# State matmuls of the SSD branch from split operands, with the operands made ahead and some work of TensorE placed elsewhere

## The chip, the cores and the metric

The kernel runs on one core of a Trainium2 chip. The metric is the device time of one execution in microseconds, as the median of several runs. One further execution is profiled; its trace has every instruction of every engine with its start and its length, and every statement on where time goes refers to that execution.

## The reference

Two layers of a hybrid encoder on 512 tokens of width 1024, all in float32. Each layer projects the residual stream x once and feeds three branches (a bidirectional Mamba-2 scan, differential attention, cross-attention into 256 memory tokens); each branch is projected back, weighted by a gate computed from x, and summed. The change touches only the first branch, and of it only the states between chunks and the order of work:

```python
# one direction; chunks of Q = 128 tokens, 32 heads in 4 groups, state width N = 128
decay_states = jnp.exp(a_cum[..., -1:] - a_cum)
states = jnp.einsum('bcqgn,bgrcq,bcqgrp->bcgrpn', bm, decay_states, xs)
chunk_decay = jnp.moveaxis(jnp.exp(a_cum[..., -1]), -1, 0)
def step(h, inp):
    s_c, d_c = inp
    return h * d_c[..., None, None] + s_c, h
_, prev = lax.scan(step, h0, (jnp.moveaxis(states, 1, 0), chunk_decay))
y_off = jnp.einsum('bcqgn,bcgrpn,bgrcq->bcqgrp', cm, prev, jnp.exp(a_cum))
```

Here `xs` is the convolved x times the step `dt`, `bm` and `cm` are the convolved B and C, and `prev` is the state in front of each chunk. It is computed forward and backward.

## The kernel before, in words

**Split operands.** Most products are made of float32 values split in two: a rounded high part h (the type `F32R`, which TensorE takes in a single pass) and the rest l. `split` makes them: ScalarE copies x to h, VectorE subtracts h from x. `mm3` then runs three matmuls, l by h, h by l and h by h, into one PSUM bank. A plain `mm` of float32 operands is one instruction in the program and two in the trace.

**Units.** The layer's weights come in units of 128 x 1024, one DMA each on the SP queue. A unit is loaded, split (`wh` on ScalarE, `wl` on VectorE) two units ahead, and used by 24 matmuls of 128 x 512 into one PSUM bank of the pool `pj`, or two banks of 12 for the branch output. `U(unit, ...)` puts a unit into TensorE's order and, in the middle of it, small pieces of other work; `J(...)` puts such a piece between units. TensorE's order is the written one; the order on the other engines is set by a scheduler that goes by priorities and its own estimates, and `late(-n)` raises the priority of what stands within.

**One group of the scan** (8 heads; g = 0 to 3) consists of:

- `bu`, `cu`, `xu(g, 0..3)`: projections of B, C and four slices of x, each convolved over five taps: one operation on ScalarE and four on VectorE (`acc`), then a SiLU on ScalarE (`bC`, `cC`, `xsC`).
- `bturn`, `xturn(g, b)`: four transposes on TensorE into the one bank of the pool `pt`, copied out by ScalarE to `bT` and `xsT`.
- `states(g, part)`, part 0 to 2: the forward state of chunk `part` and the backward one of chunk 3 - `part`. VectorE multiplies `xsT` by the weights `wst` (`xw`), TensorE multiplies that by `bT`, and the running state `prev` takes it up (ScalarE for part 0, two VectorE operations later).
- `expos(g, b)`: for two heads, tables of decays are loaded into one of two buffers (`ab`), masked on VectorE, put through eight exponentials on ScalarE, summed and multiplied by the products of B and C to give `m`; the decays `eb` are loaded as well.
- `block(g, b)`: matmuls of `prev` with `cC` and of `xsT` with `m`, then some VectorE work to the gated, split output `yh`, `yl`.
- `wu(g, 0..3)`: the branch's output projection, summed into `mrg`.
- `zu` are the units of the SiLU gate z. `gu` are early units of the branch gates: a tanh into `tg`, which is stored to DRAM for later.

While group g is projected, the blocks of the group before run in between. In what follows, the "first group" of the loop is g = 1, beside which the blocks of group 0 run.

Of the kernel before, what the change touches and what calls it, by code (L numbers as in the profile page):

```python
# [12 lines left out]
F32R = mybir.dt.float32r  # L13
# [7 lines left out]
P = 128  # L21
S = 512
# [29 lines left out]
class Net:  # L52
# [391 lines left out]
    def ssd(self, l):  # L444
# [22 lines left out]
        def bturn(g):  # L467
            pt = self.bank(self.pt, "pt")
            for c in range(4):
                self.tr(pt[:, c * P:(c + 1) * P], G["bC", g][:, c * P:(c + 1) * P])  # L470
            G["bT", g] = self.t(self.sp, [P, S], "bT")
            self.act(G["bT", g], pt)

        def cpart(g, ps=None):
            def f(wh, wl):
# [30 lines left out]
        def xturn(g, b):  # L506
# [2 lines left out]
                self.tr(pt[:, c * P:(c + 1) * P], xc[:, c * P:(c + 1) * P])  # L509
            self.act(G["xsT", g][:, :, b * P:(b + 1) * P], pt.rearrange("p (c e) -> p c e", c=4))  # L510

        def states(g, part):

            sp = self.sp
            for d, c in ((0, part), (1, 3 - part)):
                hs = slice(d * 32 + g * 8, d * 32 + g * 8 + 8)
                old = G.get(("prev", g, d, c))
                xw = self.t(sp, [P, 8, 64], "xw", bufs=2)
                self.tt(xw, G["xsT", g][:, c, :].rearrange("p (h e) -> p h e", h=8),
                        bc(self.wst[:, c, hs, None], [P, 8, 64]), ALU.mult)  # L520
                ps = self.bank(self.pm, "pm")
                self.mm(ps, G["bT", g][:, c * P:(c + 1) * P], xw)
                pv = self.t(sp, [P, 8, 64], f"prev{d}{c}")
                psv = ps.rearrange("p (h e) -> p h e", h=8)
                if old is None:
                    self.act(pv, psv)
                else:
                    self.tt(pv, old.rearrange("p (h e) -> p h e", h=8),
                            bc(self.dtot[:, c, hs, None], [P, 8, 64]), ALU.mult)
                    self.tt(pv, pv, psv, ALU.add)  # L530
                G["prev", g, d, c + 1 if d == 0 else c - 1] = pv.rearrange("p h e -> p (h e)")

        def zpart(g, b):
            def f(wh, wl):
# [104 lines left out]
        def gate(i, j, t=None):  # L639
            def f(wh, wl):  # L640
                ps = yield from self.proj2(wh, wl)
                o = self.t(self.sp, [P, S], "tg", bufs=2) if t is None else t()
                self.act(o, ps, AF.Tanh, scale=0.5, bias=self.hgb[:, 8 * i + j:8 * i + j + 1])
                if t is None:
                    d = self.dgt[i, j] = self.t(self.dp, [P, S], f"dgt{i}{j}")
# [96 lines left out]
        U(gu())  # L742
        J(xturn, 0, 3)
        J(expos, 0, 0)
        U(gu())
        J(states, 0, 0)
        U(zu(0, 0), (states, 0, 1))
        for g in range(1, 4):
            p = g - 1
            U(bu(g))  # L750
            if g == 1:
                J(states, 0, 2)
                U(zu(p, 1), (block, p, 0))
            else:
                J(block, p, 0)
                U(zu(p, 1))
            J(expos, p, 1)
            U(cu(g))
            U(gu())
            J(block, p, 1)  # L760
            U(xu(g, 0), (bturn, g))
            J(expos, p, 2)
            U(zu(p, 2), (within, g))
            U(xu(g, 1))
            J(block, p, 2)
            J(xturn, g, 0)
            U(zu(p, 3))
            J(expos, p, 3)
            U(xu(g, 2))
            J(xturn, g, 1)  # L770
            J(block, p, 3)
            U(xu(g, 3))
            U(gu(), (xturn, g, 2))
            U(wu(p, 0))
            J(xturn, g, 3)
            U(wu(p, 1))
            U(wu(p, 2), (states, g, 0))
            J(states, g, 1)
            U(wu(p, 3))
            J(states, g, 2)  # L780
            J(expos, g, 0)
            U(zu(g, 0))

        for b in range(4):
            U(gate(0, 4 + b, place(4 + b)))
# [645 lines left out]
```

## Time and profile before

| | |
|---|---|
| median of 3 runs | 2189.69 us |
| lowest and highest | 2188.62 and 2190.12 us |
| the profiled execution | 2190.09 us |
| its span, first to last instruction | 2188.3 us |
| busy, share of the span | TensorE 98%, VectorE 71%, ScalarE 53%, GpSimd 3% |
| granted TensorE clock, mean | 0.997 |
| HBM read and written | 126 GB/s |

A row of the timeline gives start and length in microseconds, engine, source line, operation, out<-in with partitions and elements, how many instructions are merged, and in brackets the idle time before it and what ended that. L99 is the line of `mm`, L77 of `tt`, L80 of `stt`, L87 of `act` and L107 of `tr`, all helpers, so the names of the tiles tell which step it is. Matmuls overlap: the length of one is longer than the step from its start to the next one's start. In a row of groups the columns are count, busy time, mean length in nanoseconds, and idle time before.

### The profile page before, as it was taken

The numbers are of one execution on the slowest core, as the hardware profiler recorded it, in microseconds if no ns is written. First come the engines' busy times: TensorE is split into PE (matmuls) and PEld (weight loads), VectorE is DVE, ScalarE is ACT, GpSimd is POOL, SyncE is SP. The second block draws the span as 40 slices with busy tenths as digits, with TensorE's granted clock in tenths as the row PEclk, the third lists the DMA queues.
The fourth block names the chain that finished last, engine by engine and source line by source line (L and its number), as shares of the span: only waits on it lengthen the run. The fifth ranks groups of instructions, "written<-read, shape, count | busy, mean of one in ns | idle before, by whom it ended". The sixth has DMA issues, their size and how long they took to land.

```text
span 2188.3 us, 29240 instructions
## 1 busy us (share of the span) xinstructions
PE 2148.1 (98%) x11122; PEld 1787.3 (82%) x11122; DVE 1546.6 (71%) x2404; ACT 1152.1 (53%) x2035; POOL 61.3 (3%) x38
## 2 busy tenths in 40 slices
PE   8999999999999999999999999999999999999998
PEld 6787878788888888887888777878788888888876
DVE  5677777869554788766566677878675547888667
ACT  5676757554432455543345676858533325555430
POOL 0010101010000000000000000101000000000000
PEclk9999999999999999999999999999999999999999
DMA  4654545454554433324564654545444334333253
GB/s 162 159 148 136 163 122 169 121 144 149 173 168 123 137 113 107 112 83 153 153 208 128 164 148 135 165 134 160 127 135 135 106 113 130 112 111 107 91 160 111
DMA packets 111984, 299.46 MB, mean 137 GB/s; under 512 B 12716, under 2 KB 13284, under 8 KB 111588
## 3 DMA queue, kind: packets, MB, share of 16 engines
q1 hardware_dynamic: 111844, 297.60, 46.0%
q8 instruction: 87, 1.43, 0.3%
q14 instruction: 53, 0.43, 0.1%
HBM read 257.16 MB, written 19.43 MB: 126 GB/s over the span
## 4 chain that ended last, share of the span: by engine, by line
PE 78%; DVE 9%; DMA 7%; ACT 2%; issue 2%; SPq 0%; DVEq 0%; ACTq 0%
PE pj L99 61%; PE pm L99 14%; DMA ab<-dab 4%; PE pt L107 2%; DVE acc L80 2%; DVE wl L77 2%; DMA wr<-wu 2%; DVE y L77 1%; DMA fth<-rd 1%; DVE eb L77 1%; ACT wh L87 1%; DVE ab L77 1%; ACT L87 1%; DVE y L80 1%; DMA mkv<-dkv 0%
## 5 line engine op out<-in xcount | busy, mean ns | idle before, releaser
L99 PE MATMUL pj<-xh,wl 128*128 128x512 f32 x1664 | 668.3, 402 | 0.2 <-DVE wl L77 0.2
L99 PE MATMUL pj<-xh,wh 128*128 128x512 f32 x1664 | 652.5, 393 | 8.1 <-ACT xh L87 6.0
L99 PE MATMUL pj<-xl,wh 128*128 128x512 f32 x1664 | 652.0, 392 | 0.0
L77 DVE TENSOR_TENSOR wl<-wr,wh 128x1024 fp32r<-128x1024 f32 x330 | 403.6, 1224 | 154.8 <-ACT wh L87 154.2
L87 ACT ACTIVATE wh<-wr 128x1024 fp32r<-128x1024 f32 x330 | 347.5, 1054 | 248.4 <-PE pj L99 169.5
L99 PEld LDWEIGHTS pj<-xh,wh 128*128 128x128 f32 x1664 | 314.0, 189 | 76.1 <-ACT xh L87 6.0
L99 PEld LDWEIGHTS pj<-xh,wl 128*128 128x128 f32 x1664 | 314.0, 189 | 70.8 <-issue 6.7
L99 PEld LDWEIGHTS pj<-xl,wh 128*128 128x128 f32 x1664 | 314.5, 189 | 65.0 <-issue 2.9
L87 ACT ACT_TABLE_LOAD x107 | 137.3, 1283 | 93.4 <-DVE ab L77 31.7
L87 ACT ACTIVATE ab<-ab,bias 128x128 f32<-128x128 f32 x512 | 161.3, 390 | 14.6 <-DVE ab L77 13.8
L80 DVE SCALAR_TENSOR_TENSOR acc<-pj,pr,acc 128x510 f32<-128x510 f32 (+1 forms) x192 | 142.2, 744 | 32.6 <-ACT acc L87 31.7
L77 DVE TENSOR_TENSOR ab<-ab,cst 128x1024 f32<-128x1024 f32 x64 | 78.2, 1223 | 72.9 <-DMA ab<-dab 72.8
L1059 DVE TENSOR_REDUCE fmx<-pm 128x1 f32<-128x512 f32 x128 | 85.0, 685 | 46.8 <-PE pm L99 46.8
L99 PE MATMUL pj<-yh,wl 128*128 128x512 f32 x256 | 106.1, 415 | 0.5 <-DVE mrg L77 0.5
L87 ACT ACTIVATE fpp<-pm,fmx 128x512 f32<-128x512 f32 x128 | 87.1, 685 | 33.8 <-DVE fmx L1059 33.8
L99 PE MATMUL pj<-dy,wh 128*128 128x512 f32 (+1 forms) x384 | 102.6, 356 | 0.9 <-DVE dy L77 0.9
L99 PE MATMUL pj<-yl,wh 128*128 128x512 f32 x256 | 100.2, 391 | 0.1
L99 PE MATMUL pj<-yh,wh 128*128 128x512 f32 x256 | 99.8, 390 | 0.0
L77 POOL TENSOR_TENSOR sqa<-sqa,sz 128x512 f32<-128x512 f32 x32 | 60.1, 1878 | 887.6 <-ACT sz L87 887.6
L99 PE MATMUL pj<-cy,wh 128*128 128x512 f32 x256 | 78.8, 389 | 0.0
L99 PEld LDWEIGHTS pj<-dy,wh 128*128 128x128 f32 x384 | 67.5, 188 | 13.2 <-DVE dy L77 2.1
L99 PE MATMUL pj<-wh,xl 128*128 128x256 f32 x256 | 73.3, 286 | 0.0
(274 smaller groups left out, 3309.2 us busy)
## 6 DMA issues: line engine op xcount, KB each, us to landing
wr<-wu SPq DMA_DIRECT2D x336, 512.0 KB, 3.7
ab<-dab SPq DMA_DIRECT2D x64, 512.0 KB, 5.6
eb<-deb SPq DMA_DIRECT2D x64, 256.0 KB, 5.9
mkv<-dkv SPq DMA_DIRECT2D x16, 512.0 KB, 4.1
rsw<-rx SPq DMA_DIRECT2D x64, 128.0 KB, 2.3
dy<-dy SPq DMA_DIRECT2D x32, 256.0 KB, 2.3
dgt<-tg SPq DMA_DIRECT2D x24, 256.0 KB, 3.9
dkv<-mo SPq DMA_DIRECT2D x16, 256.0 KB, 4.4
```

Source lines behind the costliest of these rows:

```text
L77: (eng or self.nc.vector).tensor_tensor(out=out, in0=a, in1=b, op=op)
L80: self.nc.vector.scalar_tensor_tensor(out=out, in0=a, scalar=s, in1=b, op0=op0, op1=op1)
L87: self.nc.scalar.activation(out=out, in_=a, func=f, **kw)
L99: self.nc.tensor.matmul(out=out, lhsT=a, rhs=b, start=first, stop=last)
L107: self.nc.tensor.transpose(out=out, in_=x, identity=self.ident)
L1059: nc.vector.tensor_reduce(out=mx[:, c:c + 1], in_=ps, axis=AX.X, op=ALU.min)
```

## The change

The states are no longer multiplied as plain float32. `bturn` splits the transposed B into `bTh` and `bTl`, out of the PSUM bank. A new function `weighted` makes the weighted x of both directions (in a tile of the tag `y`, which `block` uses too) and splits it into `xwh` and `xwl`, two buffers each; it stands ahead of `states` with raised priority, for part 0 behind the last transposes of the group's x, for parts 1 and 2 at the end of the part before. `states` then runs `mm3`, three single passes for each direction.

The pieces also stand elsewhere in the units. Each part of the states is now in the middle of a unit of its own, where two of three had shared a place or stood between units. The transposes of x stand later: those of slice 0 behind the z unit, of slice 1 in the middle of the last x projection, of slice 2 behind the gate unit. One early gate has gone from the last group's (g = 3) place behind `cu` to the start, ahead of the states of group 0; there are as many units as before. `tg` has one buffer instead of two.

```diff
@@ bturn
-            G["bT", g] = self.t(self.sp, [P, S], "bT")
-            self.act(G["bT", g], pt)
+            G["bT", g] = [self.t(self.sp, [P, S], n, F32R) for n in ("bTh", "bTl")]
+            self.split(*G["bT", g], pt)
@@
+        def ends(part):
+            return (0, part), (1, 3 - part)
+
+        def weighted(g, part):
+
+            with self.late(-LN):
+                for d, c in ends(part):
+                    hs = slice(d * 32 + g * 8, d * 32 + g * 8 + 8)
+                    xh, xl = G["xw", g, d] = [self.t(self.sp, [P, S], n, F32R, bufs=2) for n in ("xwh", "xwl")]
+                    xw = self.t(self.sp, [P, S], "y", bufs=2)
+                    self.tt(xw.rearrange("p (h e) -> p h e", h=8),
+                            G["xsT", g][:, c, :].rearrange("p (h e) -> p h e", h=8),
+                            bc(self.wst[:, c, hs, None], [P, 8, 64]), ALU.mult)
+                    self.split(xh, xl, xw)
+
         def states(g, part):
...
-            for d, c in ((0, part), (1, 3 - part)):
+            for d, c in ends(part):
...
-                xw = self.t(sp, [P, 8, 64], "xw", bufs=2)
-                self.tt(xw, G["xsT", g][:, c, :].rearrange("p (h e) -> p h e", h=8),
-                        bc(self.wst[:, c, hs, None], [P, 8, 64]), ALU.mult)
                 ps = self.bank(self.pm, "pm")
-                self.mm(ps, G["bT", g][:, c * P:(c + 1) * P], xw)
+                self.mm3(ps, *(t[:, c * P:(c + 1) * P] for t in G["bT", g]), *G.pop(("xw", g, d)), True, True)
...
+            if part < 2:
+                weighted(g, part + 1)
@@ gate
-                o = self.t(self.sp, [P, S], "tg", bufs=2) if t is None else t()
+                o = self.t(self.sp, [P, S], "tg") if t is None else t()
@@ the order
         J(expos, 0, 0)
+        J(weighted, 0, 0)
         U(gu())
-        J(states, 0, 0)
+        U(gu(), (states, 0, 0))
         U(zu(0, 0), (states, 0, 1))
         for g in range(1, 4):
             p = g - 1
-            U(bu(g))
+            U(bu(g), *(((states, 0, 2),) if g == 1 else ()))
             if g == 1:
-                J(states, 0, 2)
                 U(zu(p, 1), (block, p, 0))
             else:
                 J(block, p, 0)
                 U(zu(p, 1))
             J(expos, p, 1)
             U(cu(g))
-            U(gu())
-            J(block, p, 1)
-            U(xu(g, 0), (bturn, g))
+            if g < 3:
+                U(gu())
+                J(block, p, 1)
+            U(xu(g, 0), *(((block, p, 1),) if g == 3 else ()), (bturn, g))
             J(expos, p, 2)
             U(zu(p, 2), (within, g))
             U(xu(g, 1))
             J(block, p, 2)
+            U(zu(p, 3))
             J(xturn, g, 0)
-            U(zu(p, 3))
             J(expos, p, 3)
             U(xu(g, 2))
-            J(xturn, g, 1)
             J(block, p, 3)
-            U(xu(g, 3))
-            U(gu(), (xturn, g, 2))
+            U(xu(g, 3), (xturn, g, 1))
+            U(gu())
+            J(xturn, g, 2)
             U(wu(p, 0))
             J(xturn, g, 3)
+            J(weighted, g, 0)
             U(wu(p, 1))
             U(wu(p, 2), (states, g, 0))
-            J(states, g, 1)
-            U(wu(p, 3))
-            J(states, g, 2)
+            U(wu(p, 3), (states, g, 1))
             J(expos, g, 0)
-            U(zu(g, 0))
+            U(zu(g, 0), (states, g, 2))
```

The states on TensorE, part 0 of g = 1 in layer 0, in the middle of the third output unit. Before:

```order
L99 MATMUL pj_1540<-yh_875,wh_1462 128x512
L99 MATMUL pj_1540<-yl_876,wh_1462 128x512
L99 MATMUL pm_1557<-xw_1555,bT_1077 128x512
L99 MATMUL pm_1563<-xw_1561,bT_1077 128x512
L99 MATMUL pj_1541<-yh_875,wl_1463 128x512
L99 MATMUL pj_1541<-yh_875,wh_1462 128x512
```

and now:

```order
L99 MATMUL pj_1627<-yl_949,wh_1537 128x512
L99 MATMUL pm_1642<-xwh_1575,bTl_1151 128x512
L99 MATMUL pm_1642<-xwl_1576,bTh_1150 128x512
L99 MATMUL pm_1642<-xwh_1575,bTh_1150 128x512
L99 MATMUL pm_1648<-xwh_1581,bTl_1151 128x512
L99 MATMUL pm_1648<-xwl_1582,bTh_1150 128x512
L99 MATMUL pm_1648<-xwh_1581,bTh_1150 128x512
L99 MATMUL pj_1628<-yh_948,wl_1538 128x512
```

Two plain matmuls have become two times three of split operands at the same place.

The transposes of slice 2 of x on TensorE (`xsC` with the number of its slice's tile), g = 1 in layer 0, beside the early gate (`pj_1425` before, `pj_1500` now; `xh` and `xl` are the split x). Before:

```order
L99 MATMUL pj_1425<-xl_83,wh_1309 128x512
L99 MATMUL pj_1425<-xh_82,wh_1309 128x512
L107 MATMUL pt_1438<-cst_81,xsC_230_1338 128x128 x4
L99 MATMUL pj_1425<-xh_82,wl_1310 128x512
L99 MATMUL pj_1425<-xl_83,wh_1309 128x512
```

and now:

```order
L99 MATMUL pj_1500<-xl_83,wh_1384 128x512
L99 MATMUL pj_1500<-xh_82,wh_1384 128x512
L107 MATMUL pt_1529<-cst_81,xsC_250_1413 128x128 x4
L99 MATMUL pj_1541<-yh_948,wl_1452 128x512
L99 MATMUL pj_1541<-yh_948,wh_1451 128x512
```

They stood in the middle of the gate's 24 matmuls; now they stand behind all of them, ahead of the first output unit.

VectorE in layer 0 where block 2 of group 0 and a convolution of x meet (`ab` with `cst` is the mask of a freshly loaded table, `eb` and `y` are the block, `acc` the convolution). Before, around the convolution of slice 2 (`acc_1339`):

```order
L77 TENSOR_TENSOR m_1290<-ab_1278,gs_420 128x512
L77 TENSOR_TENSOR m_1305<-ab_1293,gs_420 128x512
L77 TENSOR_TENSOR wl_1310<-wr_1307,wh_1309 128x1024
L77 TENSOR_TENSOR ab_1644<-ab_1644,cst_81 128x1024
L80 SCALAR_TENSOR_TENSOR acc_1339<-pj_1313,pr_127,acc_1339 128x510
L77 TENSOR_TENSOR eb_1276<-pm_1352,eb_1276 128x384
```

and now, around the convolution of slice 1 (`acc_1277`):

```order
L77 TENSOR_TENSOR m_1365<-ab_1353,gs_422 128x512
L77 TENSOR_TENSOR ab_1368<-ab_1368,cst_81 128x1024
L77 TENSOR_TENSOR wl_1248<-wr_1245,wh_1247 128x1024
L77 TENSOR_TENSOR ab_1741<-ab_1741,cst_81 128x1024
L77 TENSOR_TENSOR eb_1174<-pm_1284,eb_1174 128x384
L80 SCALAR_TENSOR_TENSOR acc_1277<-pj_1251,pr_127,acc_1277 128x510
```

The first mask of group 1's own tables (`ab_1644` before, `ab_1741` now) stood behind both `m` of block 3 and ahead of the third convolution; now it stands ahead of the second convolution, and of block 2, with one `m` of block 3 still to come behind it.

## The prediction

> **What bounds the kernel now.** I read the page's busy times first, then the chain of waits, then who makes TensorE wait, then the timeline at those waits.
>
> ```profile
> PE 2148.1 (98%) x11122; PEld 1787.3 (82%) x11122; DVE 1546.6 (71%) x2404; ACT 1152.1 (53%) x2035; POOL 61.3 (3%) x38
> PE 78%; DVE 9%; DMA 7%; ACT 2%; issue 2%; SPq 0%; DVEq 0%; ACTq 0%
> PE pt L107 <- ACT xsC L87: 9.4, 7, 3.8
> ```
>
> TensorE is the bound: 98% of the span, and the path lies on it for 78%. So only two things can move the time: fewer or cheaper TensorE passes, and its stalls. The last row (engine that waited, what for: us, times, longest) is its longest wait, and it is in the SSD stage that the change edits: transposes of x wait for the convolved x (`xsC`). Two of the seven hold most of the time. Layer 0, then layer 1, and behind them a stretch of layer 0 with the granted clock (busy us of PE, PEld, DVE, ACT and POOL, then PEclk, DMA share, GB/s):
>
> ```profile
> 169.99 0.39 PE L99 MATMUL pj<-xh,wh 128*128 128x512 f32 x1
> 174.21 0.66 PE L107 MATMUL pt<-cst,xsC 128*128 128x128 f32 x4 [3.83 <-ACT xsC L87]
> 174.62 0.47 PE L99 MATMUL pj<-xh,wl 128*128 128x512 f32 x1
> 179.04 0.40 PE L99 MATMUL pj<-yh,wl 128*128 128x512 f32 x1
> ...
> 1307.74 0.39 PE L99 MATMUL pj<-xh,wh 128*128 128x512 f32 x1
> 1310.91 0.66 PE L107 MATMUL pt<-cst,xsC 128*128 128x128 f32 x4 [2.78 <-ACT xsC L87]
> 1311.32 0.47 PE L99 MATMUL pj<-xh,wl 128*128 128x512 f32 x1
> 1315.73 0.40 PE L99 MATMUL pj<-yh,wl 128*128 128x512 f32 x1
> ...
> 174.60:179.00 4.40, 4.40 (x15) 3.49 (x14) 4.40 (x6) 2.78 (x5) 1.31 (x1) 0.61 0.91 244
> ```
>
> A busy PE hides the second loss. Behind the first of these stalls the granted clock is 0.61 for 4.4 us; behind both, 12 matmuls take 4.42 and 4.41 us from start to start, where 12 at the usual pace (0.227 us, next rows) take 2.72. Each stall therefore costs its own length and 1.7 us more.
>
> **The change part by part.** *The states' matmuls.* Start times count here, since durations overlap:
>
> ```profile
> 83.74 0.39 PE L99 MATMUL pj<-xh,wl 128*128 128x512 f32 x1
> 87.59 0.39 PE L99 MATMUL pj<-xh,wh 128*128 128x512 f32 x1
> 87.82 1.88 PE L99 MATMUL pm<-xw,bT 128*128 128x512 f32 x4
> 89.77 0.40 PE L99 MATMUL pj<-xl,wh 128*128 128x512 f32 x1
> L99 PE MATMUL pm<-xw,bT 128*128 128x512 f32 x96 | 45.1, 591 | 0.0
> 1088.64 0.39 PE L99 MATMUL pm<-wl,wT 128*128 128x512 f32 x1
> 1091.20 0.40 PE L99 MATMUL pm<-wh,fpp 128*128 128x512 f32 x1
> ```
>
> From 87.59 to 89.77 there are the four passes of one pair of full-precision matmuls and two split ones; 2.18 - 2 x 0.227 = 1.72 us for the pair. The pace of split passes is 17 steps from 83.74 to 87.59, 0.227 us; in the other PSUM pool with new weights for each it is 11 steps from 1088.64 to 1091.20, 0.233 us. The new pair is six such passes: 1.40 us (1.36 at the quicker pace). The 96 instructions are 48 matmuls, 24 pairs: 24 x 0.32 = **7.7 us** saved (8.6 at most).
>
> *The third transpose of x and the gate.* Before, it stands in the middle of the gate that follows the fourth x projection; now behind that gate. Counted from the end of the third x projection, it falls due after transposes 0.41, a block 2.36 (158.80 to 161.92 less its wait, last rows below), 24 and 12 matmuls, 10.9 us; now after block, 24 matmuls, one set of transposes and 24 matmuls, 13.7 us. That is 2.7 us more room, less than the 3.99 us (174.21 - 169.99 - 0.23) lost in layer 0. What decides is why the convolved x is late:
>
> ```profile
> 160.76 1.22 DVE L77 TENSOR_TENSOR wl<-wr,wh 128x1024 fp32r<-128x1024 f32 x1
> 166.71 1.23 DVE L77 TENSOR_TENSOR ab<-ab,cst 128x1024 f32<-128x1024 f32 x1 [4.73 <-DMA ab<-dab]
> 167.85 0.74 DVE L80 SCALAR_TENSOR_TENSOR acc<-pj,pr,acc 128x510 f32<-128x510 f32 x1
> 173.52 0.63 ACT L87 ACTIVATE xsC<-acc 128x512 f32<-128x512 f32 x1
> DVE ab L77 <- DMA ab<-dab: 72.8, 44, 4.9
> ab<-dab SPq DMA_DIRECT2D x64, 512.0 KB, 5.6
> ```
>
> VectorE stood 4.73 us at the first mask of the next group's decay table, which waits for a load (5.6 us to land) into one of two buffers, and the convolution of the third x stood behind it. In the new order that masking stands one convolution earlier: the second x now waits behind it, and its transposes have moved from 13.7 to 18.8 us after their projection (two blocks, 60 matmuls and one set of transposes). So the third x is convolved without that wait, and both stalls go, with their slow clocks: 3.99 + 1.70 + 2.94 + 1.69 = **10.3 us** (2.94 is 1310.91 - 1307.74 - 0.23). [...]
>
> *What is late next.* The earlier masking delays block 2 of the group before, and with it `m` of block 3, where TensorE waits already; the first block of the stage waits for `prev`:
>
> ```profile
> 158.80 1.50 PE L99 MATMUL pm<-cC,prev 128*128 128x128 f32 x12
> 160.90 1.09 PE L99 MATMUL pm<-m,xsT 128*64 128x128 f32 x16 [0.59 <-DVE m L77]
> 161.92 0.50 PE L99 MATMUL pj<-xh,wl 128*128 128x512 f32 x1
> 1295.62 0.66 PE L107 MATMUL pt<-cst,xsC 128*128 128x128 f32 x4 [0.68 <-ACT xsC L87]
> 1298.64 1.10 PE L99 MATMUL pm<-m,xsT 128*64 128x128 f32 x16 [1.03 <-DVE m L77]
> 108.55 0.71 PE L99 MATMUL pm<-cC,prev 128*128 128x128 f32 x4 [0.77 <-DVE prev L77]
> 1244.86 0.94 PE L99 MATMUL pm<-cC,prev 128*128 128x128 f32 x6 [0.77 <-DVE prev L77]
> 291.81 0.66 PE L107 MATMUL pt<-cst,xsC 128*128 128x128 f32 x4 [1.08 <-ACT xsC L87]
> ```
>
> At block 3 of the first group 0.59 + 0.68 + 1.03 = 2.3 us are lost now over both layers. The mask put ahead adds 1.2 us and up to 5.6 - 2.45 = 3.1 us of load wait (a mask and a weight split stand between the freed buffer and it); the second set of transposes, no longer ahead of block 3, takes away 0.4 us of cover; against it, VectorE no longer arrives there with a backlog. I take 1.8 us in each layer, midway between the ends, 3.6 in all: **1.3 us more than now**. Ends: 0 (a gain of 2.3) and 3.5 in each layer, which with a slow clock of 1.7 is a loss of 8.1. The first block: the last states now stand 24 matmuls ahead of it (5.4 us) instead of 12, and the wait is 0.77 us; both go, **1.5 us**. The fourth transposes have the other four of the seven waits, 9.4 - 3.83 - 2.78 - 0.68 = 2.1 us, 291.81 the longest. They keep their distance to their projection: nothing, ends 2.1 less and 2.1 more.
>
> *The operands made ahead.* Each pair adds two copies on ScalarE and two subtractions on VectorE, each group one subtraction for B. Prices from like shapes:
>
> ```profile
> L77 DVE TENSOR_TENSOR xw<-xsT,wst 128x512 f32<-128x512 f32 x48 | 32.3, 686 | 6.8 <-PE pm L99 4.9 <-ACT xsT L87 1.9
> L77 DVE TENSOR_TENSOR kl<-rx,k 128x512 fp32r<-128x512 f32 x16 | 11.1, 692 | 8.2 <-ACT k L87 8.2
> L87 ACT ACTIVATE k<-rx 128x512 fp32r<-128x512 f32 x32 | 18.4, 623 | 21.9 <-DVE rx L77 21.9
> dgt<-tg SPq DMA_DIRECT2D x24, 256.0 KB, 3.9
> 1427.00:1452.00 25.00, 24.56 (x100) 17.96 (x99) 22.86 (x32) 14.77 (x33) 0.00 (x0) 1.00 0.38 118
> ```
>
> 56 subtractions of 0.69 and 48 copies of 0.62 are 39 and 30 us, all beside TensorE, so I cost them at nothing. The cover: from the fourth transposes to the first states lie 36 matmuls, 8.2 us; the chain copy out, product, copy, two subtractions and a weight split between is 0.62 + 2 x 0.69 + 0.62 + 2 x 0.69 + 1.22 = 5.2 us. For the second and third part the buffer is free only when the pair before has run: two copies and two subtractions, 2.6 us, and up to three other operations (2.1) before 24 matmuls (5.4) are over. Slack 3.0 and 0.7 us; the second is thin, and the last row (VectorE busy 22.86 of 25 us around the states of layer 1's group 2) says that six subtractions more, 4.1 us, fill that stretch entirely. What waits behind a late subtraction is the weight split for two units on, and that has a unit to spare. B's transposed bank is held 0.7 us longer; its next user is two units away. One buffer for the stored gates makes a tanh wait for the store before; gates stand at least 24 matmuls, 5.4 us, apart, and a store has landed 3.9 us after its issue: nothing, or a tanh that starts some tenths late on an engine that is not the bound.
>
> Sum: 7.7 + 10.3 + 1.5 - 1.3 = 18.2 us. The profiled execution took 2190.09 us around its span of 2188.3, 0.40 above the median of the runs, 2189.69. So 2171.9 in its terms, and **2171.5 us** as a median.
>
> **The rivals.** *The freed time is lost at the next wait.* The two stalls come back as waits of block 3 for `m`, or at the third transposes after all, because the loads, not TensorE, set the pace of the decay tables. For it: 44 VectorE waits for these loads. Against it: the masks wait at a place with more room. Then 7.7 + 1.5 stay and of the 10.3 a loss of 8.1 in other places is taken: 9.2 + 10.3 - 8.1 = 11.4 us at the mild end (2178), 9.2 alone at the other (2180.5). Chance 0.2.
>
> *The passes are not cheaper.* By mean durations a full-precision matmul is two instructions of 591 ns, 1182, and three split ones of 394 ns are also 1182. If the durations and not the starts are the cost, the 7.7 us vanish: 2179. The starts speak against it. Chance 0.04.
>
> *Everything fits.* Block 3 and the fourth transposes wait no more, and passes run at 0.227: 0.9 + 1.3 + 2.3 + 2 more, 2165. Chance 0.12.
>
> *Slower: VectorE becomes the bound in the states' units.* For groups 2 and 3 a unit with states holds a weight split of 1.22 and ten operations of 0.69 (two sums into the branch, four on the state, two products, two subtractions): 8.1 us, against TensorE's 24 x 0.227 + 1.40 = 6.85. With a decay operation and an `m` between (1.4) the excess is 2.65 us in each of the 16 second and third parts: 42 us lost against 18 won, 2214. It decides from an excess of 18.2 / 16 = 1.1 us. Against it: in 1427 to 1452 VectorE was busy 22.86 of 25 us and TensorE did not wait, and the units between groups have idle VectorE time. Chance 0.05.
>
> **How the numbers follow.** The forecast has 0.59, the rivals 0.2, 0.04, 0.12 and 0.05. Its own range is 2167 to 2176 (block 3 from 0.5 to 3.5 us, passes at either pace). The range for 8 in 10 runs from 2164, just beyond the case in which everything fits, to 2182, beyond the lost-again case. A change under 0.2% (4.4 us) cannot be told from none in this kernel. Faster by more than that: all cases but the last, 0.95, less 0.04 for what I have not seen, 0.91; within, 0.04; slower, 0.05.
>
> **What would show it.** Right: pairs of states at 1.4 us from start to start; no transpose of x waiting over 1 us in the first group, and no clock under 1.0 there; `prev` gone from TensorE's waits. Wrong: a wait on `xwl` or `xwh` above 1 us at `pm`; a wait for `m` above 2.8 us, with a slow clock behind it; wider VectorE gaps on `ab<-dab`.

## The result, and the profile after

| | before | with the change |
|---|---|---|
| median of 6 runs beside each other | 2189.90 us (2188.62 to 2192.14, and one of 4343.41) | 2177.88 us (2176.69 to 2182.81) |
| ratio, 95% interval | | 0.9947, 0.9936 to 0.9958 |
| the profiled execution, its span | 2190.09, 2188.3 us | 2179.63, 2177.9 us |
| granted TensorE clock, mean | 0.997 | 0.996 |

The change makes the kernel 0.53% faster, some 12 us (10.4 between the two spans). The ratio is of the fast runs alone, without the one of 4343.41 us. The forecast was 18.2 us less and 2171.5 us. 2177.9 lies inside the range for 8 in 10 runs (2164 to 2182), outside the forecast's own (2167 to 2176), and at the mild end of the first rival (2178).

The first part of the page after, and who makes TensorE wait (times and longest, in us):

```profile
PE 2138.8 (98%) x11170; PEld 1798.1 (83%) x11170; DVE 1582.4 (73%) x2460; ACT 1171.3 (54%) x2079; POOL 63.1 (3%) x38
PE pm L99 <- DVE m L77: 6.7, 2, 3.5
PE pj L99 <- ACT yh L87: 5.0, 2, 3.2
PE pm L99 <- DVE prev L77: 0.3, 1, 0.3
```

The waits for `xsC`, 9.4 us before, are gone, and `prev` nearly so. In their place stand `m` with 6.7 us, where 1.6 were, and a wait that was not in the list at all: `yh`. TensorE's timeline after, a pair of states, then block 3 of group 0 in both layers:

```profile
89.25 0.39 PE L99 MATMUL pm<-xwh,bTl 128*128 128x512 f32 x1
...
90.38 0.39 PE L99 MATMUL pm<-xwh,bTh 128*128 128x512 f32 x1
90.61 0.39 PE L99 MATMUL pj<-xh,wl 128*128 128x512 f32 x1
...
160.29 1.50 PE L99 MATMUL pm<-cC,prev 128*128 128x128 f32 x12
165.32 1.72 PE L99 MATMUL pm<-m,xsT 128*64 128x128 f32 x16 [3.54 <-DVE m L77]
...
1294.89 1.49 PE L99 MATMUL pm<-m,xsT 128*64 128x128 f32 x16 [3.18 <-DVE m L77]
```

A pair takes 90.61 - 89.25 = 1.36 us instead of 1.72. Counted from the last matmul before the wait to the start behind it, less the usual step, `m` costs 3.70 us in layer 0 and 3.35 in layer 1. The second new wait is at the end of the stage, where the projection of group 3 needs the `yh` of its last block. Layer 1, before and after:

```profile
1608.41 1.50 PE L99 MATMUL pm<-cC,prev 128*128 128x128 f32 x12
...
1628.89 1.05 PE L99 MATMUL pm<-cst,rs_y 128*128 128x128 f32 x8
```

```profile
1591.16 1.50 PE L99 MATMUL pm<-cC,prev 128*128 128x128 f32 x12
1601.16 0.50 PE L99 MATMUL pj<-yh,wl 128*128 128x512 f32 x1 [3.17 <-ACT yh L87]
...
1617.99 1.05 PE L99 MATMUL pm<-cst,rs_y 128*128 128x128 f32 x8
```

When TensorE starts the last block of layer 1 it is 1608.41 - 1591.16 = 17.25 us ahead of the kernel before; at the norm's last matmuls only 1628.89 - 1617.99 = 10.90 are left. In layer 0 the same two places give 471.71 - 461.60 = 10.1 and 492.19 - 484.08 = 8.1 us. So 8.35 us are lost at the ends of the two stages. 5.3 us of them are the two waits (1.97 and 3.33, counted as above); most of the rest is the clock. The slow stretches of the profile after (start and end of the kernel left out), with busy us of PE, PEld, DVE, ACT and POOL, then the granted clock, DMA share and GB/s:

```profile
165.63:169.04 3.41, 3.41 (x20) 2.69 (x16) 3.41 (x6) 1.66 (x2) 2.43 (x1) 0.50 0.93 222
1295.44:1298.85 3.41, 3.41 (x16) 2.59 (x13) 3.41 (x6) 1.41 (x2) 2.19 (x1) 0.50 0.93 213
1602.64:1609.47 6.83, 6.83 (x22) 5.47 (x21) 3.31 (x10) 1.06 (x1) 0.42 (x1) 0.50 0.30 94
```

Before, there were two stretches of 3.41 us at a granted clock of 0.50 (from 175.44 and 1312.07 us), now there are three, one of double length.

Why `m` and `yh` are late is in VectorE's rows, and one of ScalarE. First around block 3 of group 0 in layer 0:

```profile
150.35 1.23 DVE L77 TENSOR_TENSOR ab<-ab,cst 128x1024 f32<-128x1024 f32 x1 [1.76 <-DMA ab<-dab]
154.60 1.23 DVE L77 TENSOR_TENSOR ab<-ab,cst 128x1024 f32<-128x1024 f32 x1 [1.88 <-DMA ab<-dab]
155.45 3.91 ACT L87 ACTIVATE ab<-ab,bias 128x128 f32<-128x128 f32 x13
162.63 1.29 DVE L77 TENSOR_TENSOR ab<-ab 128x512 f32<-128x512 f32 x2
164.49 1.29 DVE L77 TENSOR_TENSOR m<-ab,gs 128x512 f32<-128x512 f32 x2
```

The mask of 150.35 is block 3's; that of 154.60, which waits 1.88 us for its load, belongs to the next group, whose `m` TensorE wants at 218.53. The exponentials are done by 159.4, yet the sum comes at 162.63: block 2's own operations and a convolution fill VectorE between. Then the last block of layer 1:

```profile
1590.95 0.69 DVE L77 TENSOR_TENSOR m<-ab,gs 128x512 f32<-128x512 f32 x1
1594.49 1.22 DVE L77 TENSOR_TENSOR wl<-wr,wh 128x1024 fp32r<-128x1024 f32 x1 [2.18 <-ACT wh L87]
1595.63 1.01 DVE L77 TENSOR_TENSOR eb<-pm,eb 128x384 f32<-128x384 f32 x2
1596.56 1.22 DVE L77 TENSOR_TENSOR wl<-wr,wh 128x1024 fp32r<-128x1024 f32 x1
1597.69 0.74 DVE L80 SCALAR_TENSOR_TENSOR y<-xsC,pr,pm 128x512 f32<-128x512 f32 x1
1600.38 0.72 ACT L87 ACTIVATE yh<-y,pr 128x512 fp32r<-128x512 f32 x1 [4.40 <-DVE y L77]
```

TensorE has finished the block at 1593.7, but VectorE works on it from 1595.63 only, behind a weight split that waits for ScalarE, and with a second split in between. The block's `m` is done at 1591.64 and its `yh` at 1601.1, 9.5 us later.

### The profile page after: what moved, and what is told of

Read it like the earlier page. It is cut to its first block, busy times and chain, and to the rows that moved or that the text cites. A ratio compares the mean times of both kernels' runs of the same rounds, so it can differ in the third digit from the quotient of the medians.

```text
span 2177.9 us, 29440 instructions
## 1 busy us (share of the span) xinstructions
PE 2138.8 (98%) x11170; PEld 1798.1 (83%) x11170; DVE 1582.4 (73%) x2460; ACT 1171.3 (54%) x2079; POOL 63.1 (3%) x38
## 4 chain that ended last, share of the span: by engine, by line
PE 79%; DVE 9%; DMA 8%; issue 2%; ACT 2%; SPq 0%; DVEq 0%; ACTq 0%
PE pj L99 62%; PE pm L99 14%; DMA ab<-dab 4%; PE pt L107 3%; DMA wr<-wu 2%; DVE wl L77 2%; DVE ab L77 1%; DVE y L77 1%; DVE acc L80 1%; ACT wh L87 1%; DMA fth<-rd 1%; DVE eb L77 1%; DVE m L77 1%; DVE y L80 0%; PE pt L99 0%
## 5 line engine op out<-in xcount | busy, mean ns | idle before, releaser
L77 DVE TENSOR_TENSOR ab<-ab,cst 128x1024 f32<-128x1024 f32 x64 | 78.1, 1221 | 54.1 <-DMA ab<-dab 54.1
L99 PEld LDWEIGHTS pj<-dy,wh 128*128 128x128 f32 x384 | 67.5, 188 | 13.5 <-DVE dy L77 2.4
```

The lines of the kernel that those rows point to most:

```text
L77: (eng or self.nc.vector).tensor_tensor(out=out, in0=a, in1=b, op=op)
L99: self.nc.tensor.matmul(out=out, lhsT=a, rhs=b, start=first, stop=last)
```

## The experiments

All kernels were timed against the kernel before. An overview first; the waits in us are those of TensorE in the profiled execution, layer 0 / layer 1, counted from start to start, less the usual step; "-" is under 0.5. Waits of 0.5 to 0.8 us for `xwl` in the kernels with the hold are left out.

| kernel | median | ratio, 95% interval | `m`, group 0 | `yh` at the end | other new wait |
|---|---|---|---|---|---|
| the change, again | 2177.60 | 0.9948, 0.9935 to 0.9961 | 3.80 / 3.33 | 2.40 / 1.76 | |
| operands only | 2195.98 | 1.0030, 1.0018 to 1.0042 | 7.31 + 1.81 / 7.26 + 1.81 | - / 0.65 | `xsC` of groups 2 and 3, 4.88 / 5.18 |
| order only | 2184.45 | 0.9986, 0.9977 to 0.9994 | - / - | - / 0.93 | `tg` 3.70 / 3.99 |
| gate back | 2183.01 | 0.9973, 0.9962 to 0.9984 | 1.87 + 4.42 / 1.97 + 4.41 | 0.65 / - | `xwl` 1.12 / 1.12 |
| filler | 2185.01 | 0.9984, 0.9975 to 0.9993 | 1.11 / - | 1.98 / 1.88 | `tg` 3.08 / 2.71 |
| not raised | 2176.82 | 0.9943, 0.9930 to 0.9957 | 1.60 / - | 2.08 / 1.84 | operands 2.36 / 3.17 |
| tables first | 2179.67 | 0.9964, 0.9950 to 0.9977 | - / - | 1.94 / 2.28 | `xsC`, `tg` 4.42 / 5.43 |
| hold | 2174.22 | 0.9939, 0.9927 to 0.9952 | 0.74 / 2.15 | 1.88 / 2.52 | `acc` 0.83 / - |
| hold, gate in group 2 | 2180.38 | 0.9971, 0.9960 to 0.9982 | 0.77 / 1.41 | 3.23 / 0.80 | `cC` 1.92 / 2.40, `m` of group 2 1.49 / 0.88, `acc` 0.83 / 0.79 |
| the same, tables first | 2177.65 | 0.9950, 0.9938 to 0.9962 | - / - | 1.66 / 1.81 | `cC` 2.75 / 1.96, `m` of group 2 1.41 / -, `acc` 0.91 / 1.62 |
| hold, tables first | 2174.60 | 0.9941, 0.9928 to 0.9953 | - / - | 1.20 / 3.38 | `acc` 0.85 / 1.96 |
| the same, last block early | 2171.03 | 0.9919, 0.9905 to 0.9933 | - / - | - / - | `m`: end 0.75 / 2.02, group 1 1.49 / -; `acc` 1.07 / 2.09 |

**Operands only.** The change with TensorE's order of before, and `weighted` for part 0 behind the fourth transposes; one of the places:

```diff
-            U(xu(g, 3), (xturn, g, 1))
-            U(gu())
-            J(xturn, g, 2)
+            U(xu(g, 3))
+            U(gu(), (xturn, g, 2))
...
```

> Only the operands: states from split operands made ahead, everything on TensorE in the order of before. Theory A (the decay tables set the pace, and the new order spent their lead over TensorE): the passes give their 7.7 us, the two stalls at the third transposes of x stay with their slow clocks, block 3's wait for `m` stays near 1 us and the stage's end has no wait for `yh` above 0.5 us; 2180 to 2183. Theory B (the operands themselves, raised in VectorE's order, hold the tables up): waits for `m` above 3 us or for `yh` above 1.5 us appear here too; 2185 to 2190. If the passes are not cheaper: 2188 to 2190 without a new wait.

Slower than before, beyond either theory. Of the two, B names the place: blocks 2 and 3 of group 0 wait for `m`, 17.5 us in all. Before, the first mask of block 1 stood at 101.60 on VectorE; here the same mask comes at 112.06, though its load was under way at 95.93. The rows of before, then of this kernel:

```profile
101.60 1.22 DVE L77 TENSOR_TENSOR ab<-ab,cst 128x1024 f32<-128x1024 f32 x1
```

```profile
PE pm L99 <- DVE m L77: 17.5, 4, 7.1
112.06 1.22 DVE L77 TENSOR_TENSOR ab<-ab,cst 128x1024 f32<-128x1024 f32 x1
150.91 0.70 PE L99 MATMUL pm<-m,xsT 128*64 128x128 f32 x4 [7.15 <-DVE m L77]
```

The operands are not free: they push the decay tables of the first group back by 10 us. Behind the long waits there are slow stretches too (the granted clock is 0.74 from 145 to 165 us), five times 3.41 us in all where there were two.

**Order only.** The change with full-precision states and the product made in `states`, as before:

```diff
-        J(weighted, 0, 0)
-            J(weighted, g, 0)
-                self.mm3(ps, *(t[:, c * P:(c + 1) * P] for t in G["bT", g]), *G.pop(("xw", g, d)), True, True)
+                self.mm(ps, G["bT", g][:, c * P:(c + 1) * P], xw)
```

> Only the order: full-precision states as before, everything on TensorE in the order of the change. Theory A: the stalls at the third transposes go, and block 3 of the first group waits 3 to 4 us for `m` with a slow clock behind it, and the stage's end 2 to 3 us for `yh`, as in the changed kernel: 2184 to 2187. Theory B: without the operands the tables are in time, `m` waits under 2 us and `yh` under 0.5: 2178 to 2181.

Again B on `m`: without the operands `m` of block 3 is done at 155.61, 6.91 us before TensorE asks for it. But the time is nearly A's, since a wait that neither theory had takes the place, at a bank that the tanh of a gate still has to read:

```profile
154.93 0.68 DVE L77 TENSOR_TENSOR m<-ab,gs 128x512 f32<-128x512 f32 x1
162.52 0.66 PE L99 MATMUL pm<-m,xsT 128*64 128x128 f32 x8
180.53 0.67 ACT L87 ACTIVATE tg<-pj,hgb 128x512 f32<-128x512 f32 x1
181.25 0.50 PE L99 MATMUL pj<-yh,wl 128*128 128x512 f32 x1 [3.54 <-ACT tg L87]
165.00:185.00 20.00, 16.46 (x76) 13.07 (x75) 18.79 (x24) 18.49 (x31) 1.95 (x2) 1.00 0.57 175
```

The last row: from 165 to 185 us VectorE is busy for 18.79 and ScalarE for 18.49 of 20 us. In the same window the kernel before has 17.04 and 14.50, the change 17.36 and 14.45, so "full" fits this kernel better than those two. The loss per layer in this stretch is 4.75 and 4.97 us before (0.76 at `m` and 3.99 at `xsC`; 0.83 + 1.20 + 2.94), 3.70 and 3.35 with the change, 3.70 and 3.99 here, whichever tile TensorE waits for. That made theory D of the next experiments: VectorE and ScalarE have too much to do there. The end of the stage is nearly free of a wait (`yh` under 0.5 and 0.93 us), though the gate is moved here too. And the two halves do not add up: one alone costs 0.3%, the other gains 0.14%, together they gain 0.53%.

**Gate back.** The change with the moved gate in the last group again:

```diff
-        U(gu())
         U(gu(), (states, 0, 0))
...
-            if g < 3:
-                U(gu())
-                J(block, p, 1)
-            U(xu(g, 0), *(((block, p, 1),) if g == 3 else ()), (bturn, g))
+            U(gu())
+            J(block, p, 1)
+            U(xu(g, 0), (bturn, g))
```

> The change with the moved gate put back into the third group, so that TensorE reaches the last group's blocks 5.4 us later. Theory C (the moved gate is what makes the stage's end wait for `yh`): the two `yh` waits of 1.97 and 3.32 us and the slow clock of 3.4 us behind the second go, 8 us; at the stage's start the first states lose 24 matmuls of cover and may wait up to 1.5 us for their operands or `prev` in each layer: 2170 to 2173; block 3 of the first group still waits 3 to 4 us for `m`. If the gate is not the cause the `yh` waits stay above 1.5 us: 2177 to 2181.

C is right on the place: `yh` falls to 0.65 us and less. Its price is elsewhere: at the start the tables now lack the cover of that gate, and `m` costs 12.7 us in four waits. The gate in front of the first states is what pays for the operands: `m` of the first block is ready 6.8 us ahead of TensorE, against 13.5 with the change. The time, 2183.0 us, lies above both ranges.

**Filler.** Twelve passes whose result is overwritten, inside the wait for `m`:

```diff
             py = self.bank(self.pm, "pm")
+            if (g, b) == (0, 3):
+                for _ in range(12):
+                    self.mm(py, self.xh[:, 0, :P], self.xh[:, 0, :])
```

> The change with 12 passes (128x512, their result is overwritten) put between the two halves of block 3 of the first group, where TensorE waits 3.70 and 3.35 us for `m`: 12 x 0.227 = 2.7 us of work that nobody needs. If the idle time is what brings the slow clock: about 1.0 and 0.6 us of the waits are left, the half clock behind both goes, and the kernel is 3.4 us faster with more work, 2174 to 2175.5. If the slow clock does not hang on the idle time: no change, 2177 to 2179. If the passes are paid in full: 2183.

```profile
161.31 2.98 PE L99 MATMUL pm<-xh 128*128 128x512 f32 x12
165.24 1.09 PE L99 MATMUL pm<-m,xsT 128*64 128x128 f32 x16 [0.95 <-DVE m L77]
183.36 0.80 PE L99 MATMUL pj<-yh,wl 128*128 128x512 f32 x1 [2.92 <-ACT tg L87]
165.20:169.00 3.80, 3.76 (x28) 3.09 (x29) 3.80 (x6) 2.10 (x3) 2.88 (x1) 1.00 0.92 254
182.73:189.55 6.82, 6.19 (x15) 4.89 (x16) 3.65 (x6) 6.49 (x10) 0.00 (x0) 0.50 0.68 189
```

On the spot it does what was expected: `m` comes at the same time, 1.1 us of the wait are left, and the half clock behind it is gone (1.00 from 165.20 to 169.00 us, against 0.56 in the same stretch of the change). Yet the kernel is 7 us slower than the change. The scheduler also answered the added work: on ScalarE it put an exponential of the next group's tables, with its table loads (1.28 us each), ahead of what block 3 and the transposes wait for, and the loss came back at `tg`. As a test of the clock's price the run is spoilt; that at this place the half clock went with the idle time, it shows.

**Not raised.** The operands at their own place in the order:

```diff
-            with self.late(-LN):
+            with self.late(0):
```

> The change with the operations that make the states' operands at their own place in the order instead of 300 instructions ahead of it. Theory B (the raised operands hold the decay tables up on VectorE and ScalarE): the tables of the last group get their lead back, the wait for `yh` at the stage's end falls from 1.97 and 3.32 us under 1 us and its slow clock goes, and block 3 of the first group waits for `m` under 2 us; 2168 to 2173, unless the states' matmuls now wait for `xwl`, 0.5 us or more in many of the 24 pairs. Theory D (in the stretch from block 2 of the first group to the fourth transposes VectorE and ScalarE have more to do than TensorE's pace allows, and some 4 us are lost there whichever consumer comes first; before 4.75 and 4.97 us, the change 3.70 and 3.35, the order alone 3.70 and 3.99): the stall of 3 to 4 us in each layer stays at `m`, or turns up at `tg` or `xsC`; 2174 to 2178.

```profile
PE pj L99 <- ACT yh L87: 3.6, 2, 1.9
PE pm L99 <- ACT xwh L87: 3.2, 2, 2.0
```

No difference from the change that the runs can tell. The tables of the first group are earlier (`m` of block 2 is ready 6.83 and 6.99 us ahead, against 2.95 and 2.35), and `m` gains what the first states lose to their operands; `yh` stays. So the priority decides where the loss stands, and lowering it does not take the loss away.

**Tables first.** The tables of block 3 of group 0 asked for before block 2:

```diff
+            if g == 1:
+                J(expos, p, 3)
             J(block, p, 2)
             U(zu(p, 3))
             J(xturn, g, 0)
-            J(expos, p, 3)
+            if g > 1:
+                J(expos, p, 3)
```

> The change with the decay tables of block 3 of the first group asked for before block 2 instead of after it, so that their sum and `m` stand ahead of block 2's own operations on VectorE. If `m` is late only because of its place in VectorE's order: the waits of 3.70 and 3.35 us go with their slow clocks, 10.4 us in all, and the kernel takes 2167 to 2170. Theory D (VectorE and ScalarE are full in this stretch): the wait for `m` goes, and 2.5 to 4 us per layer are lost a few us later, at `tg`, `xsC` or `yh`; 2174 to 2181.

```profile
177.97 1.11 PE L107 MATMUL pt<-cst,xsC 128*128 128x128 f32 x4 [2.55 <-ACT xsC L87]
183.59 0.50 PE L99 MATMUL pj<-yh,wl 128*128 128x512 f32 x1 [1.55 <-ACT tg L87]
```

As D said: `m` no longer waits, and 4.4 and 5.4 us are lost some 15 us later. One place is traded for another.

**Hold.** The next group's first tables held out of the stretch, by a copy that makes their load wait:

```diff
+                if (g, b) == (1, 0):
+                    self.act(ab[:, 0, 0, 0:1], G["xsT", g][:, 0, 256:257])
                 src = self.dab.rearrange("(d h) q -> h d q", d=2)[h:h + 1]
```

> The change with the first decay tables of the second group held back: a copy of one column of x's transpose is written into their buffers before the load, so that load, mask, exponentials, sum and `m` of that group (wanted 25 us after they are ready) can't come before the third transposes of x. Theory D: this takes two masks, a sum and an `m` (1.13 + 1.13 + 0.6 + 0.6 = 3.5 us) off VectorE and 13 exponentials and a table load off ScalarE in the stretch, and the wait for `m` falls from 3.70 and 3.35 us to under 1 us without another wait of over 1.5 us taking its place; the slow clocks behind it go: 2167 to 2171, if the `yh` waits stay as they are. If the stretch is not full but `m` is paced by its own load: the `m` wait stays above 2.5 us, 2176 to 2180.

```profile
PE pm L99 <- DVE m L77: 2.5, 2, 2.0
PE pj L99 <- ACT yh L87: 4.1, 2, 2.4
```

The wait for `m` falls from 6.7 to 2.5 us, and this time nothing above 0.83 us takes its place in the stretch. By the ratios (0.9939 and 0.9948) the kernel is some 2 us faster than the change, less than the 7 to 11 expected, and the two intervals overlap: layer 1 keeps 2.15 us and its slow clock.

**Hold, with the gate taken from group 2 instead of group 3**, and **the same with the tables first**:

```diff
-            if g < 3:
+            if g != 2:
                 U(gu())
                 J(block, p, 1)
-            U(xu(g, 0), *(((block, p, 1),) if g == 3 else ()), (bturn, g))
+            U(xu(g, 0), *(((block, p, 1),) if g == 2 else ()), (bturn, g))
```

> The change with the second group's first tables held back, and the gate that the change takes out of the last group taken out of the group before it instead. If the last group's tables fall behind because TensorE got there one gate (5.4 us) early: `m` of the last group's first block is ready over 20 us ahead instead of 11.8, the last block's some 6 us ahead instead of 2.4 and 1.7, and the two waits for `yh` (1.88 and 2.52 us with the first change alone) fall under 0.7 us: 2170 to 2172, against 2174 without the second edit. Rival: the third group now loses what the last one lost, since its fourth block has `m` only 3.4 us ahead: waits for `m` of 1.5 us or more there, 2174 to 2177.

> As the one before, and with the tables of block 3 of the first group asked for before block 2. With the order alone changed this only moved the loss (waits of 2.7 and 1.7 us at `xsC` and `tg`), which I put down to a full VectorE. If that is right, the 3.5 us taken off VectorE by holding the next tables back now leave room: the remaining waits for `m` (0.74 and 2.15 us, and one slow clock) go, and those at `xsC` and `tg` stay under 1 us each: 2166 to 2169. If VectorE was not the reason: `xsC` and `tg` wait 2 us or more again, 2171 to 2176.

```profile
PE pm L99 <- ACT cC L87: 4.0, 2, 2.2
PE pm L99 <- DVE m L77: 3.9, 4, 1.3
PE pj L99 <- ACT yh L87: 3.7, 2, 3.1
```

The first goes the way of its rival, in place and not in size: TensorE is 5.4 us early one group sooner and waits there, for `cC`, which the rival did not name, and for `m`; the time, 2180.4 us, is above the rival's 2174 to 2177. `yh` did not go, though `m` of the last block is ready 3.6 and 6.0 us ahead; what that depends on stands below, under the end of the stage. In the second the waits for `m` of group 0 go, as expected, and `xsC` and `tg` stay short, but `acc` waits 0.91 and 1.62 us there and the later groups keep their waits; the time is above both ranges.

**The change again**, beside these two:

> The change as it is, as the yardstick for the two kernels beside it: 2176 to 2180, with the waits for `m` of 3.3 to 3.7 us and for `yh` of 2 to 3.3 us.

The time is as expected (first row of the table); of the waits, 3.80 us at `m` and 1.76 at `yh` lie just outside what was expected.

**Hold and tables first, the gates as in the change**, and **the last block in the middle of the last gate**:

```diff
-            U(gate(0, 4 + b, place(4 + b)))
-            J(block, 3, b)
+            if b < 3:
+                U(gate(0, 4 + b, place(4 + b)))
+                J(block, 3, b)
+            else:
+                U(gate(0, 4 + b, place(4 + b)), (block, 3, b))
```

> The change with the second group's first tables held back and the tables of block 3 of the first group asked for before block 2, the gates where the change has them. The full VectorE (theory D) says: of the 2174.2 us with the hold alone, the waits for `m` of 0.74 and 2.15 us and the one slow clock (1.7 us) go, and nothing above 1.7 us takes their place in the first group, as beside it in the kernel with the gate moved; the `yh` waits of some 1.9 and 2.5 us stay: 2169 to 2172. If the loss only moves: `tg` or `xsC` at 2 us or more, 2173 to 2176.

> As the one before, and the last block of the stage put into the middle of the last gate instead of behind it, so that 12 passes, 2.7 us, lie between that block and the product that needs its `yh`. In VectorE's order the last block's own operations then stand ahead of the weight split that now stands between them, 1.1 us. If `yh` is late because the last block's chain of VectorE and ScalarE operations starts too late behind TensorE's block: the two `yh` waits (1.9 and 2.5 us) go below 0.5 us, `m` of that block, ready some 2 us ahead, waits under 1 us: 3 to 5 us less than the kernel before it, 2165 to 2169. If the chain is set by ScalarE and the loads and not by when TensorE comes: the wait stays, at `yh` or at `m`, within 1 us of the kernel before it.

The first is no faster than the hold alone: the wait for `m` is gone, but 1.96 us at a bank that VectorE still has to read (`acc`) and 3.38 us at `yh`, both in layer 1, take up the gain, each with a slow stretch of 3.41 us behind it. That is the rival's range, with another tile. The second removes `yh`. The rows of its last block, to be read beside those of the change above:

```profile
1589.33 1.09 PE L99 MATMUL pm<-m,xsT 128*64 128x128 f32 x16 [1.85 <-DVE m L77]
1593.16 1.01 DVE L77 TENSOR_TENSOR eb<-pm,eb 128x384 f32<-128x384 f32 x2
1594.10 0.74 DVE L80 SCALAR_TENSOR_TENSOR y<-xsC,pr,pm 128x512 f32<-128x512 f32 x1
1597.56 0.50 PE L99 MATMUL pj<-yh,wl 128*128 128x512 f32 x1
```

The weight split between `eb` and `y` is gone, 1.1 us, and 12 passes of the gate, 2.7 us, cover the chain; the two changes came together, so their shares are worked out and not tested. 2171.0 us is 3.6 less than the kernel before it, as expected, though not as low as 2169; its interval (0.9905 to 0.9933) lies below that of the change (0.9935 to 0.9961), so this version beats both kernels. `m` of that block waits in return (0.75 and 2.02 us).

## Why the prediction was right, and where it was wrong

The sign and the range for 8 in 10 runs held, and so did both gains: cheaper passes, and no stall at the third transposes. The account of what they would cost did not hold: a price of 1.3 us was forecast for the wait behind them, and 7.7 and 8.35 us went at two waits. The time is that of the first rival (chance 0.2) rather than of the forecast. Without 6.1 us of gains that were not forecast (3.3 at the fourth transposes, 1.4 and 1.4 below) it would be above 2182, so that it lies in the range is in part luck. Step by step, with what the two profiled executions show (faster by, in us):

| step | forecast | measured |
|---|---|---|
| passes of the states | 7.7, at most 8.6 | 24 x (1.72 - 1.36) = 8.6 |
| third transposes, with two slow clocks | 10.3 | 10.3 |
| wait for `m` at block 3 | -1.3 (ends 2.3 and -8.1) | 2.8 - 7.05 - 3.4 = -7.7 |
| first block, `prev` | 1.5 | 1.86 - 0.74 = 1.1 |
| fourth transposes | 0 (ends -2.1 and 2.1) | 2.7, and 0.6 behind one of them |
| operands, made ahead | 0 | at `m` and `yh` |
| end of the stage, `yh` | not seen | -8.35 |

Up to the last block of each stage TensorE had gained 10.1 us in layer 0 and 17.25 - 8.7 = 8.6 in layer 1 (1139.44 against 1148.12 at its start): 18.7, close to the forecast's 18.2 by errors that cancel. The table's rows above the last give 15.6; 1.4 us come from the start of the kernel (below), and 1.4 from the steps at the transposes of x (64 in each layer, 6.40 and 6.46 us before, 5.74 and 5.75 now). At the end 8.35 go.

*Passes.* Mis-sized by the choice of pace: behind split passes a pair runs at 0.227 us a pass, the quicker of the two rows. The rival "the passes are not cheaper" falls: 1.36 us for a pair against 1.72.

*Third transposes.* Right in size: no `xsC` wait in the list. But the cause was only half of it. I blamed the place of one mask in VectorE's order. Before, with the change and with the order alone the stretch loses 3.35 to 4.97 us per layer, at `xsC`, `m` or `tg`; with the tables first 4.4 and 5.4. Two things lowered the sum: work taken out of the stretch (hold), and a TensorE that comes later because it has waited at the first states (not raised). A stall was moved 13 us ahead in the order of work (160.90 against 174.21 us in the profile before), not removed. That a full VectorE is the reason is what the hold supports, without settling it: its time was 3 us above the range of theory D.

*Wait for `m`.* The step that failed most in size. I took the middle between the ends, and it came out near the bad one. The price was worked out from the moved mask, its load and the lost cover. By how far `m` is ready ahead of TensorE it has two parts. From block 2 to block 3 the lead falls by 6.65 and 5.70 us with the change and by 6.67 and 6.47 with the order alone, where it fell by 2.62 and 1.50 before: that part, some 4 us a layer, is the new order's, and the forecast's bad end had 3.5. The other part is what is left at block 2: 13.58 and 12.71 us with the order alone, 2.95 and 2.35 with the operands in it. So without the operands and with the same order `m` of block 3 is ready 6.9 us ahead, with them it is 3.7 us late.

*Operands cost nothing.* The step that failed in kind. I gave the cover of each operand (36 and 24 matmuls) and was right that no states' matmul waits for `xwl`. I asked what a late operand holds up, and not what the operands hold up: the decay tables behind them on VectorE. In the first group the operands alone show it (the masks 10 us later, above). In the last group it takes both halves of the change: `m` of its first block was ready 39 us ahead before, 37.7 with the operands alone, 27.6 with the order alone, 11.8 with the change. In that group the tables take longer for a block than TensorE's 13.47 us, before as after (in layer 0 of the change `m` of blocks 1 to 3 is ready at 430.6, 446.2 and 460.7 us, 15.6 and 14.5 apart; before, 16.5 and 15.6), so TensorE catches up. At the last block the lead is 2.3 and 0.9 us with the change, and 5.3 to 6.9 before and with either half alone.

*End of the stage.* Not in the prediction. The moved gate was counted as cover for the first states only; the gate back shows that it also brings TensorE to the last block 5.4 us early, and takes `yh` along. The first rival's mechanism, freed time lost at the next wait, thus holds in two places, one of which it did not name.

What makes `yh` late can be read from all the traces together. In the seven kernels with the order of VectorE shown above (the change, the same again, filler, not raised, tables first, hold, hold with tables first) `yh` of the last block is done 9.45 or 9.46 us behind its `m`, in both layers of each, while it comes anything from 5.3 to 7.5 us behind TensorE's block. So a chain on ScalarE and VectorE that begins beside `m` sets it (in layer 1 of the change a table load of 1.28 us, copies of weights of 1.05 us and splits of 1.22 us each, the block's own operations), and not the time at which TensorE comes. This is read from the fixed distance; no run moved `m` of that block alone. In the other order (operands only, order only, gate back, both kernels with the gate taken from group 2) a product and a copy of the block before stand behind `m`, and the chain takes 11.97 to 12.03 us. `m`'s lead and the wait for `yh` sum to 4.25 to 4.27 us in the first order and, where the wait is over 0.5 us, to 6.78 or 6.79 in the second: 2.29 + 1.97 and 0.94 + 3.33 with the change, 3.55 + 3.23 and 5.99 + 0.80 with the gate taken from group 2. Before, TensorE's block set the pace: `yh` came 4.03 us behind it in both layers. The last kernel shortened the chain to 8.32 us and let TensorE need `yh` 2.7 us later.

Of what would show it: pairs at 1.4 us, no `xsC` wait and `prev` almost gone came true, and VectorE's gaps for the loads of the tables became narrower (72.8 us before, 54.1 after). A full clock in the first group did not come true, and a wait for `m` above 2.8 us with a slow clock, named as wrong, did.

## What to carry to other kernels

When work is put on an engine that is "not the bound", ask which of its other products come later for it, and by how much they lead now; the cover of the new work itself is the smaller half of the question. A stall that goes away in one order and returns at another tile can be a sign of a stretch in which other engines have too much to do: move work that is not wanted yet out of it, and compare sums of waits, not single ones. Where the last step of a stage hangs on a chain of two other engines, measure from which product the chain keeps a fixed distance: that product has to come earlier, or the chain be made shorter, and work of the first engine's own can cover what is left.

## What was not expected of the hardware

The half clock came in pieces of 3.41 us. In the profiled execution of the change the three slow stretches (granted clock 0.50) begin at 165.63, 1295.44 and 1602.64 us, 331.0 and 90.0 times 3.413 us apart, and last 3.41, 3.41 and 6.83 us; before, two of 3.41 us begin at 175.44 and 1312.07 us, 333.0 times 3.413 us apart. The waits ahead of these five end between 0.31 and 1.48 us before them, so the steps are not those of the waits. In pieces of 3.41 us counted from these starts, the first and last 20 us left out, TensorE was idle for 1.98 to 3.10 us in the one ahead of each slow stretch, and for at most 1.64 us in any that had no half clock behind it. Idle time is not all of it: the stretch at 1602.64 is two pieces long though TensorE was busy for all of its 6.83 us, and that of the filler from 182.73 to 189.55 though it was idle for only 0.63 us. Why stays open. With the hold alone, 2.15 us of waiting cost a slow stretch, and 2.52 us that lie across a border of two pieces (idle for 1.04 and 1.38 us) did not; so in these executions the price of a stall hung on where it fell. The rows show the slow stretch behind the first, then the two pieces that share the second, whose border is 89.0 times 3.413 us behind 1292.81:

```profile
1292.81:1296.22 3.41, 3.41 (x13) 2.51 (x10) 2.82 (x4) 2.01 (x3) 0.83 (x1) 0.50 0.72 211
1593.18:1596.59 3.41, 2.37 (x11) 1.64 (x9) 3.31 (x6) 0.00 (x0) 0.00 (x0) 1.00 0.87 283
1596.59:1600.00 3.41, 2.03 (x7) 1.10 (x8) 2.03 (x4) 1.31 (x3) 1.29 (x1) 1.00 0.85 330
```

The start of the kernel fits the same steps: matmuls of 512 columns step by 0.43 us until 15.05 us before and until 12.18 us after, and by 0.23 from there; the two places lie 47.0 and 45.0 times 3.413 us ahead of the first slow stretch of their execution. The first matmuls start at 6.02 and 6.16 us, so the 2.9 us less at half pace are the 1.4 us above, and that they come from the change is not shown. The half clock may also spread the times of one kernel: the filler took 2180.2 us in an execution with a mean clock of 0.998 and 2188.8 in one with 0.993, but 2189.3 in one with 0.996, so the clock is not all of that.
